# Loading the branch results into the place of their second part, and splitting them there

## The chip, the cores and the metric

The kernel runs on one core of a Trainium2 chip. The core has a matrix engine (TensorE, PE in the profile), a vector engine (DVE), a scalar engine (ACT), a general engine (POOL) and a sync engine (SP), which here issues nearly all transfers. Each engine works through its own list of instructions in order; semaphores join the lists. The metric is the device time of one execution in microseconds (us), lower is better: the median of three runs is 1705.68 us (1704.77 to 1709.62).

## The reference

The reference is one block of a network on 1024 tokens of width 1024. What matters here is its end:

```python
y_a = hm * jax.nn.sigmoid(a_o) * jax.nn.silu(a_z)               # first branch, [1024, 1024]
y_b = att.reshape(B, S, DA_WIDTH) * jax.nn.silu(b_z)            # second branch, [1024, 1024]
mix = (jax.nn.sigmoid(g_a + gb[0]) * jnp.einsum('bsc,cd->bsd', y_a, w_branch_a[layer])
       + jax.nn.sigmoid(g_b + gb[1]) * jnp.einsum('bsc,cd->bsd', y_b, w_branch_b[layer]))
x = x + jnp.einsum('bsd,de->bse', mix, w_out[layer])
return rmsnorm(x, final_g)
```

Before it stand a projection of the normed input, a gated recurrence (the first branch) and an attention with two softmaxes (the second).

## The kernel before, in words

All matrix products are made in three terms: each operand is split into a first part H, rounded to the short format that PE takes, and a second part L = value − H, and the product is H·H + H·L + L·H. So every operand needs a cast on ACT (H) and a subtraction on DVE or POOL (L).

Both branches leave their results transposed in device memory, as eight tiles of 128 features by 1024 tokens each: `yb0` to `yb7` for the second branch (in the profile `yb`, numbered 90 to 97) and `ya0` to `ya7` for the first (82 to 89). The **mixing** reads them back. `load_y` (L1310 to L1316) loads one tile of 512 KB into a tile `yraw`, which has two places in turn, takes two lasting places H and L, casts `yraw` to H on ACT (L1314) and subtracts on DVE (L1315). The lasting places are called `sl_yb` (a set of sixteen) and `sl_r` (another sixteen, in memory that the normed input `hH`, `hL` held until the last projection).

`mix_units` then makes eight output tiles per branch. For each, two halves of 512 tokens; each half is a group of 24 matmuls on PE (L429 in `proj`): for k from 0 to 7 the three terms with H and L of tile k. Two PSUM banks `pj` take turns. The branch b comes first ("pass B"), its groups are evicted by DVE at L1339; branch a follows ("pass A"). The places change hands: `ya0` to `ya3` go into `sl_r`, but `ya4` to `ya7` go into places of `sl_yb` that pass B has just finished with, and so do the first parts of the output matrix `w_out` (`load_wo`, from L1357), whose rows also come by way of the two places of `yraw`.

Around these loads other work shares the queues. The last gate products (`hH`, `hL` with `wH`, `wL`) run on PE until the mixing begins; ACT evicts them (L837, tile `gt`) and SP stores them (`tga`, 256 KB each). Every 10.9 us a weight tile `raw` (512 KB) is loaded, cast on ACT (L204, `wH`) and subtracted on POOL (L209, `wL`); the load of the next one waits for POOL. A tile `tgl` (512 KB) brings back the gate for each output tile.

PE's list is in the order in which the program writes it. The lists of SP, ACT, DVE and POOL in this stage are put in order when the program is built, by a scheduler that plans with its own costs and with what is free when; so a change to what a load waits for can move other instructions too. A transfer in SP's list that waits holds up all that stand behind it.

Of the kernel before, what the change touches and what calls it, by code (L numbers as in the profile page):

```python
# [7 lines left out]
F32 = mybir.dt.float32  # L8
# [6 lines left out]
S = 1024  # L15
# [4 lines left out]
L = 256  # L20
# [89 lines left out]
class Block:  # L110
# [1197 lines left out]


    def load_y(self, src, i, slot):  # L1310
        raw = self.wy.tile([128, S], F32, name="yraw", tag="yraw", bufs=2)
        self.q.dma_start(out=raw, in_=src[i])
        h, l = slot("H"), slot("L")
        self.a.copy(h, raw)  # L1314
        self.v.tensor_tensor(out=l, in0=raw, in1=h.bitcast(F32), op=ALU.subtract)  # L1315
        return h, l  # L1316

    def slot(self, which, dt=F32R):
        pool, bufs = {"yb": (self.wy, 16), "mb": (self.wy, 8), "r": (self.wr, 16)}[which]
        return pool.tile([128, S], dt, name="sl_" + which, tag=which, bufs=bufs)  # L1320
# [320 lines left out]
```

## Time and profile before

| what | value |
|---|---|
| median of three runs | 1705.68 us |
| the profiled execution's own time | 1706.56 us |
| its span, first to last instruction | 1704.7 us |
| PE busy | 1654.3 us, 97% |
| DVE, ACT, POOL busy | 988.3, 777.0, 606.5 us |
| mean granted TensorE clock | 0.994 |
| last matmul of the gate products starts at | 1426.42 us |
| first matmul of pass B starts at | 1427.42 us |
| first matmul of pass A starts at | 1521.95 us |

Times inside the execution count from the span's start. A row of the timeline has start, duration, engine, line, operation, output<-inputs, and in brackets the idle time before it with what ended that. A row of the stretches has their bounds and length, each engine's busy time with its count of instructions, the granted TensorE clock as a share of full speed, the transfer engines' busy share and the GB/s moved.

### The profile page before, as it was taken

How to read it: one execution, taken by the hardware profiler on the slowest of the kernel's cores; microseconds unless marked ns; L12 is line 12 of the kernel's file. 1: busy time of each engine (PE TensorE's matmuls, PEld its weight loads, DVE VectorE, ACT ScalarE, POOL GpSimd, SP SyncE). 2: the span in 40 equal slices, each digit the busy share in tenths (PEclk: the TensorE clock that was granted, in tenths of full speed). 3: DMA queues.
4: the chain of work that ended last, by engine and by line, in shares of the span. 5: the costliest groups of instructions: out<-in, count | busy, mean ns of one | idle time of the engine just before them, and what ended most of it. 6: DMA issues, size and time to landing. Idle time of an engine off the chain costs nothing. (4 is left out here: it accounts for less than half of the span.)

```text
span 1704.7 us, 25425 instructions
## 1 busy us (share of the span) xinstructions
PE 1654.3 (97%) x9431; PEld 1389.8 (82%) x9431; DVE 988.3 (58%) x1799; ACT 777.0 (46%) x1554; POOL 606.5 (36%) x680
## 2 busy tenths in 40 slices
PE   7999999999999999999999999999999899999998
PEld 5777887887877987898788878899999777888887
DVE  5778668674377666666666655226666633135533
ACT  7454555553265455454545455325655644022221
POOL 5767676665243134413241331221330312212000
PEclk9999999999999999999999999999999999999999
DMA  5334444334231213221231222175464327344222
GB/s 181 98 121 130 137 123 132 116 124 146 65 81 44 63 38 87 56 69 38 75 81 32 62 62 75 50 208 155 143 170 137 109 89 237 117 147 136 87 91 83
DMA packets 175630, 178.79 MB, mean 105 GB/s; under 512 B 12185, under 2 KB 135410, under 8 KB 175506
## 3 DMA queue, kind: packets, MB, share of 16 engines
q1 hardware_dynamic: 174594, 175.58, 34.5%
q8 instruction: 74, 1.21, 0.3%
q10 hardware_dynamic: 912, 1.59, 0.2%
q14 instruction: 50, 0.41, 0.1%
HBM read 114.11 MB, written 46.24 MB: 94 GB/s over the span
## 5 line engine op out<-in xcount | busy, mean ns | idle before, releaser
L429 PE MATMUL pj<-hH,wH 128*128 128x512 f32 x640 | 266.8, 417 | 3.3 <-ACT f L542 1.5
L429 PE MATMUL pj<-hH,wL 128*128 128x512 f32 x640 | 252.0, 394 | 1.8 <-POOL wL L207 1.8
L429 PE MATMUL pj<-hL,wH 128*128 128x512 f32 x640 | 250.8, 392 | 0.2 <-DVE hL L580 0.2
L209 POOL TENSOR_TENSOR wL<-raw,wH 128x1024 fp32r<-128x1024 f32 x41 | 99.7, 2431 | 291.9 <-ACT wH L204 289.5
L928 ACT ACTIVATE e<-S,nm 128x1024 f32<-128x1024 f32 x128 | 142.5, 1115 | 96.1 <-DVE nm L926 96.0
L926 DVE TENSOR_REDUCE nm<-S 128x1 f32<-128x1024 f32 x128 | 150.5, 1218 | 8.5 <-PE S L923 7.8
L429 PEld LDWEIGHTS pj<-hH,wH 128*128 128x128 f32 x640 | 121.0, 189 | 37.9 <-issue 14.5
L451 PE MATMUL pj<-wH,hH 128*128 128x256 f32 x512 | 149.9, 293 | 0.3
L948 DVE TENSOR_TENSOR pL<-T,pH 128x512 fp32r<-128x512 f32 x128 | 87.9, 689 | 105.8 <-ACT pH L947 104.9
L451 PE MATMUL pj<-wL,hH 128*128 128x256 f32 x512 | 144.8, 283 | 1.4 <-POOL wL L207 1.4
L429 PEld LDWEIGHTS pj<-hH,wL 128*128 128x128 f32 x640 | 120.6, 188 | 30.3 <-POOL wL L207 3.2
L451 PE MATMUL pj<-wH,hL 128*128 128x256 f32 x512 | 144.5, 282 | 0.0
L429 PEld LDWEIGHTS pj<-hL,wH 128*128 128x128 f32 x640 | 121.3, 190 | 18.3 <-DVE hL L580 0.6
L429 PE MATMUL pj<-sl_yb,wH 128*128 128x512 f32 x384 | 121.8, 397 | 4.4 <-ACT sl_yb L1314 2.2
L947 ACT CAST pH<-T 128x512 fp32r<-128x512 f32 x128 | 74.8, 585 | 84.6 <-PE T L131 84.0
L204 ACT CAST wH<-raw 128x1024 fp32r<-128x1024 f32 x56 | 58.9, 1052 | 114.3 <-PE pj L429 88.1
L923 PE MATMUL S<-kst,qq 64*128 64x512 f32 x768 | 106.7, 408 | 0.0
L451 PEld LDWEIGHTS pj<-wH,hH 128*128 128x128 f32 x512 | 97.7, 191 | 5.5 <-issue 2.2
L451 PEld LDWEIGHTS pj<-wL,hH 128*128 128x128 f32 x512 | 97.5, 190 | 2.3 <-POOL wL L207 2.3
L451 PEld LDWEIGHTS pj<-wH,hL 128*128 128x128 f32 x512 | 97.7, 191 | 0.1
L429 PEld LDWEIGHTS pj<-sl_yb,wH 128*128 128x128 f32 x384 | 73.3, 191 | 22.5 <-DVE sl_yb L1315 3.3
L923 PEld LDWEIGHTS S<-kst,qq 64*128 64x128 f32 x768 | 67.8, 184 | 26.3 <-issue 10.5
(358 smaller groups left out, 4112.2 us busy)
## 6 DMA issues: line engine op xcount, KB each, us to landing
raw<-in_w_in_dram SPq DMA_DIRECT2D x88, 512.0 KB, 3.9
kst<-hl SPq DMA_DIRECT2D x64, 128.0 KB, 2.4
qq<-hl SPq DMA_DIRECT2D x64, 128.0 KB, 2.4
x<-in_x_dram SPq DMA_DIRECT2D x8, 512.0 KB, 6.1
cak<-y SPq DMA_DIRECT2D x16, 256.0 KB, 2.3
cakH<-cin SPq DMA_DIRECT2D x16, 256.0 KB, 4.4
cakL<-tz SPq DMA_DIRECT2D x16, 256.0 KB, 4.1
gm<-oz SPq DMA_DIRECT2D x16, 256.0 KB, 2.7
```

The source lines that it names most:

```text
L204: self.a.copy(wH, raw)
L209: self.p.tensor_tensor(out=wL, in0=raw, in1=wHf, op=ALU.subtract)
L429: self.t.matmul(ps, lhsT=l[:, k, :], rhs=r, start=(n == 0), stop=(n == 23))
L451: self.t.matmul(ps[:, i, :], lhsT=l, rhs=r[:, k, :], start=(kh == 0 and k == 0 and m == 0), stop=(kh == 1 and k == 3 and m == 2))
L923: self.t.matmul(ps[:, o], lhsT=qq[r, x, c], rhs=k[r, y, o], start=(m == 0), stop=(m == 2))
L926: v.tensor_reduce(out=nm, in_=ps, axis=AX.X, op=ALU.max, negate=True)
L928: a.activation(out=e, in_=ps, func=AF.Exp, bias=nm[:, 0:1], accum_out=Z[:, j, t:t + 1])
L947: a.copy(pH[:, :, s], ps)
L948: v.tensor_tensor(out=pL[:, :, s], in0=ps, in1=pH[:, :, s].bitcast(F32), op=ALU.subtract)
```

## The change

`load_y` no longer has a tile `yraw`. It takes the two lasting places first, loads the tile straight into the place of L (seen as 32-bit floats), casts from there to H on ACT, and subtracts on DVE in place: L = L − H. `load_wo` is as before and now has the two places of `yraw` for itself until the output stage.

```diff
     def load_y(self, src, i, slot):
-        raw = self.wy.tile([128, S], F32, name="yraw", tag="yraw", bufs=2)
+
+        h, l = slot("H"), slot("L")
+        raw = l.bitcast(F32)
         self.q.dma_start(out=raw, in_=src[i])
-        h, l = slot("H"), slot("L")
         self.a.copy(h, raw)
         self.v.tensor_tensor(out=l, in0=raw, in1=h.bitcast(F32), op=ALU.subtract)
         return h, l
```

A load therefore waits for the place of its L, and no longer for the subtraction of the tile two before it. For `yb0` to `yb7` and `ya0` to `ya3` these places are free early. For `ya4` to `ya7` the place is that of L of `yb0` to `yb3`, which the last group of pass B still reads: each of these loads now waits for a matmul of that group. Lines after it stand one further down (L1314 is the load, L1315 the cast, L1316 the subtraction, L1367 the load of `w_out`).

The number of instructions on each engine stays; PE's list does not change but for the names of the tiles. The other lists move, at three places. The rows are: line, operation, output<-inputs, shape.

**SP, the loads of the second branch's tiles, from the fifth (`yb_94`) to the first of the next branch.** Before:

```order
L1312 DMA yraw<-yb_94 128x1024
L838 DMA tga_72<-gt 128x512
L1312 DMA yraw<-yb_95 128x1024
L838 DMA tga_73<-gt 128x512
L1312 DMA yraw<-yb_96 128x1024
L1312 DMA yraw<-yb_97 128x1024
L838 DMA tga_73<-gt 128x512
L173 DMA raw<-in_w_branch_b_dram 128x8x128
L1312 DMA yraw<-ya_82 128x1024
```

Now:

```order
L1314 DMA sl_yb<-yb_94 128x1024
L838 DMA tga_73<-gt 128x512
L1367 DMA yraw<-in_w_out_dram 128x1024
L1314 DMA sl_yb<-yb_95 128x1024
L1314 DMA sl_r<-ya_82 128x1024
L838 DMA tga_73<-gt 128x512
L1314 DMA sl_yb<-yb_96 128x1024
L173 DMA raw<-in_w_branch_b_dram 128x8x128
L1314 DMA sl_r<-ya_83 128x1024
L1314 DMA sl_yb<-yb_97 128x1024
```

The last three tiles of the second branch now stand behind a row block of `w_out` and two tiles of the first branch, `yb_97` also behind the weight `raw`, and `yb_95` and `yb_96` each behind a store of gates. Another row block of `w_out` stands further up, ahead of `yb_93`; and `yb_91` moved behind the weight `raw` that it was ahead of.

**ACT, the casts of the same tiles and what lies between them**, from the weight before the third cast on. Before:

```order
L204 CAST wH<-raw 128x1024
L1314 CAST sl_yb<-yraw 128x1024
L837 ACTIVATE gt<-pj,gbh 128x512
L1314 CAST sl_yb<-yraw 128x1024 x2
L837 ACTIVATE gt<-pj,gbh 128x512
L1314 CAST sl_yb<-yraw 128x1024
```

Now:

```order
L204 CAST wH<-raw 128x1024
L837 ACTIVATE gt<-pj,gbh 128x512
L1315 CAST sl_yb<-sl_yb 128x1024 x2
L837 ACTIVATE gt<-pj,gbh 128x512
L1315 CAST sl_yb<-sl_yb 128x1024
```

The second eviction shown used to have five casts ahead of it and has four now, since the eviction before it has moved ahead of the third cast. Further down (not shown) the casts into `sl_r` stand between those of the last three tiles of `sl_yb`.

**SP, the last tiles of the first branch, at the change from pass B to pass A.** Before (`ya_86` and `ya_87` stand some twelve rows further up):

```order
L173 DMA raw<-in_w_branch_a_dram 128x8x128
L1312 DMA yraw<-ya_88 128x1024
L1312 DMA yraw<-ya_89 128x1024
L1327 DMA tgl<-tga_67 128x1024
L173 DMA raw<-in_w_branch_a_dram 128x8x128
L1366 DMA yraw<-in_w_out_dram 128x1024 x4
```

Now:

```order
L173 DMA raw<-in_w_branch_a_dram 128x8x128
L1314 DMA sl_yb<-ya_86 128x1024
L1314 DMA sl_yb<-ya_87 128x1024
L1328 DMA tgl<-tga_67 128x1024
L1314 DMA sl_yb<-ya_88 128x1024
L173 DMA raw<-in_w_branch_a_dram 128x8x128
L1314 DMA sl_yb<-ya_89 128x1024
L1367 DMA yraw<-in_w_out_dram 128x1024 x3
```

All four loads now stand here; `ya_88` is behind the gate tile `tgl` and `ya_89` behind the weight `raw` as well, both of which they were ahead of.

## The prediction

> **What bounds the kernel now.** I read the page first, then the stretches of the mixing stage, then the chain of waits from its start to pass A. The page's first lines:
>
> ```profile
> span 1704.7 us, 25425 instructions
> PE 1654.3 (97%) x9431; PEld 1389.8 (82%) x9431; DVE 988.3 (58%) x1799; ACT 777.0 (46%) x1554; POOL 606.5 (36%) x680
> ```
>
> PE is the bound, so the change is worth what it does to PE's stops. The stretches of the stage (columns: bounds, length, busy time of PE, PEld, DVE, ACT, POOL, granted clock, share of the transfer engines, GB/s):
>
> ```profile
> 1410.00:1420.00 10.00, 10.00 (x46) 8.29 (x45) 3.44 (x2) 5.04 (x6) 2.40 (x1) 1.00 0.82 290
> 1430.00:1431.00 1.00, 1.00 (x7) 0.81 (x6) 0.00 (x0) 0.20 (x1) 1.00 (x1) 1.00 0.89 356
> 1430.00:1440.00 10.00, 6.58 (x20) 4.10 (x19) 3.14 (x3) 3.31 (x4) 2.17 (x1) 0.79 0.86 268
> 1432.36:1435.77 3.41, 1.23 (x3) 0.48 (x3) 1.23 (x1) 1.10 (x2) 0.00 (x0) 1.00 0.92 311
> 1435.77:1442.60 6.83, 6.14 (x14) 4.48 (x15) 3.58 (x4) 2.27 (x3) 0.00 (x0) 0.50 0.59 190
> 1442.60:1446.00 3.40, 3.40 (x16) 2.79 (x15) 0.79 (x2) 0.19 (x1) 0.00 (x0) 1.00 0.69 240
> 1460.00:1510.00 50.00, 50.00 (x223) 41.40 (x222) 6.19 (x9) 4.22 (x4) 9.77 (x5) 1.00 0.31 97
> ```
>
> There is one real stop, at the start of pass B. PE is busy for 1.23 of the 3.41 us before 1435.77, and then the clock stands at 0.50 for 6.83 us: with 6.14 us of matmuls in them that costs some 3.07 us more. Later, as in 1460 to 1510, PE never stops, so what is gained or lost at the stop reaches the end. The transfer engines are nearly full around the stop: 290, 268 and 311 GB/s at shares of 0.82 to 0.92. The chain of waits across the stop (start, duration, what):
>
> ```profile
> 1427.61 1.06 ACT sl_yb L1314
> ...
> 1428.69 1.24 DVE sl_yb L1315
> ...
> 1429.95 4.93 DMA yraw<-yb
> ...
> 1434.90 1.05 ACT sl_yb L1314
> ...
> 1435.98 1.24 DVE sl_yb L1315
> 1437.21 0.04 issue
> 1437.26 81.91 PE pj L429 x350
> ```
>
> This is the chain of two places: the sixth tile's subtraction frees a place of `yraw`, the eighth tile's load starts at 1429.95 and lands at 1434.88, cast and subtraction follow, and PE has k = 7's second part at 1437.26. The whole stop's size comes from these rows:
>
> ```profile
> 1426.42 0.39 PE L429 MATMUL pj<-hH,wL 128*128 128x512 f32 x1
> 1427.42 0.73 PE L429 MATMUL pj<-sl_yb,wH 128*128 128x512 f32 x2 [0.61 <-ACT gt L837]
> ...
> 1445.99 0.69 DVE L1339 SCALAR_TENSOR_TENSOR sl_mb<-tgl,pj 128x512 f32<-128x512 f32 x1 [2.61 <-PE pj L429]
> ...
> 1516.51 0.62 PE L429 MATMUL pj<-sl_yb,wH 128*128 128x512 f32 x2
> ...
> 1521.95 0.62 PE L429 MATMUL pj<-sl_r,wH 128*128 128x512 f32 x2
> ```
>
> A half, 24 matmuls, takes 1521.95 − 1516.51 = 5.44 us, 0.227 each. Without a stop the second half would be evicted 48 matmuls after 1426.42, at 1426.42 + 10.88 + 0.42 = 1437.7 (0.42 is one matmul's 0.39 and the start of DVE). It is evicted at 1445.99. So 8.3 us is all that better loads could win here.
>
> **The change: the work itself.** The same sixteen loads, casts and subtractions:
>
> ```profile
> L1312 SPq DMA_DIRECT2D yraw<-yb x8: 320/320/417, 1403.2 to 1429.9; - x8
> L1314 ACT CAST sl_yb<-yraw x8: 1041/1048/1057, 1407.1 to 1434.9; 128x1024 fp32r<-128x1024 f32 x8
> L1315 DVE TENSOR_TENSOR sl_yb<-yraw,sl_yb x8: 1216/1225/2630, 1408.2 to 1436.0; 128x1024 fp32r<-128x1024 f32 x8
> L1342 DVE TENSOR_TENSOR sl_mb<-sl_mb,tgl 128x512 f32<-128x512 f32 x16 | 12.9, 807 | 0.5
> L1341 DVE SCALAR_TENSOR_TENSOR tgl<-tgl,pj 128x512 f32<-128x512 f32 x16 | 11.0, 687 | 25.2 <-PE pj L429 25.2
> ```
>
> (The first three rows: one tile's instructions with shortest, median and longest in ns; the last two: groups with mean ns.) No row shows a subtraction of this shape in place. The nearest, L1342, is an addition in place: 807 ns mean for half the size, not faster and at most 17% slower than its neighbour L1341. I take 0, ends 0 and 0.2 us for each of the two on the path.
>
> **First place: pass B's tiles.** What the old chain made late is no longer tied to two places. But the new list of SP puts more ahead of the eighth tile: its own queue becomes the wait. (Timeline rows, and last a row of transfers issued, here `ya_88` and `ya_89`: count, size, median us to landing.) From the weight load at 1408.48 on:
>
> ```profile
> 1408.48 0.38 SPq L173 DMA_DIRECT2D raw<-in_w_branch_b_dram  x1
> 1408.95 0.53 SPq L1327 DMA_DIRECT2D tgl<-tgb  x1
> ...
> 1429.69 2.48 POOL L209 TENSOR_TENSOR wL<-raw,wH 128x1024 fp32r<-128x1024 f32 x1 [10.36 <-ACT wH L204]
> ...
> yraw<-ya SPq DMA_DIRECT2D x2, 512.0 KB, 3.5
> ```
>
> the list up to and with `yb_97` holds three `raw`, seven tiles of the second branch, two `tgl`, two blocks of `w_out` and two tiles of the first branch, sixteen loads of 0.524 MB, and four stores of 0.262 MB: 9.44 MB. A load alone lands 3.5 us after its issue, of which 1.8 us are its bytes at 290 GB/s, so bytes flow from about 1408.5 + 1.7 = 1410.2. At 311 GB/s, the rate of the stretch in which the engines were fullest, 9.44 MB take 30.4 us: `yb_97` lands at about 1440.6. No gap opens before that, by this replay: `yb_93` lands at 1410.2 + 3.93 MB / 311 = 1422.8, its cast and the eviction behind it release a store, and `w_out`, `yb_95` and `ya_82` issue at about 1425, while older bytes last to 1427.
>
> Cast (1.05) and subtraction (1.22) make k = 7's second part ready at 1442.9, 5.6 us later than the 1437.26 of before. From there 26 matmuls and the eviction's 0.4 take 6.3 us at full clock, and about 1.5 us more, since after so long a stop the half clock lasts to about 1446 (the stretches above change at steps of 3.41 us). Before it was 1445.99 − 1437.26 = 8.7. **Term: 5.6 + 7.8 − 8.7 = +4.7 us.**
>
> Bounds. At 356 GB/s, the best single microsecond, the load lands at 1436.7, k = 7 is ready at 1439.0, 1.7 late, and half clock to 1442.6 adds 1.8 to the 6.3: +1.1. At 268 GB/s it lands at 1445.4: 10.4 late, plus 6.3 and up to 1.7 of clock, less 8.7: +9.7. With an empty queue it still could not land early: it stands behind `raw`, which waits for POOL's `wL`, whose cast waits for the last gate matmul at 1426.2 + 0.4; 1.05 and 2.4 us later it is 1430.1, two more issues at 0.47 make 1431.0, after the old 1429.95. Landing 3.5 later, it would be ready at 1436.8: −0.4.
>
> The Trainium skill's "DMA: Bandwidth & Descriptors" (Specifications) gives about 358 GB/s as what one core gets from device memory. Only the one microsecond at 356 reaches that here; with it as the steady rate the term would be an estimated +1.
>
> **Second place: `ya4` to `ya7`.** Before, the first two tiles were split and the other two on their way when pass A began (timeline rows, a row of the tile `yraw`'s instructions with first and last start, and a row of transfers issued):
>
> ```profile
> 1521.97 1.05 ACT L204 CAST wH<-raw 128x1024 fp32r<-128x1024 f32 x1 [2.80 <-issue]
> ...
> 1522.15 0.69 DVE L1339 SCALAR_TENSOR_TENSOR sl_mb<-tgl,pj 128x512 f32<-128x512 f32 x1 [1.54 <-PE pj L429]
> ...
> 1523.10 2.41 POOL L209 TENSOR_TENSOR wL<-raw,wH 128x1024 fp32r<-128x1024 f32 x1 [8.48 <-ACT wH L204]
> ...
> 1526.64 0.50 PE L429 MATMUL pj<-sl_yb,wH 128*128 128x512 f32 x1 [0.22 <-DVE sl_yb L1315]
> ...
> 1527.77 0.50 PE L429 MATMUL pj<-sl_yb,wH 128*128 128x512 f32 x1 [0.17 <-DVE sl_yb L1315]
> ...
> L1312 SPq DMA_DIRECT2D yraw<-ya x2: 319/320/320, 1519.5 to 1520.6; - x2
> ...
> yraw<-in_w_out_dram SPq DMA_DIRECT2D x2, 512.0 KB, 5.4
> ```
>
> PE stopped for 0.22 and 0.17 us at k = 6 and 7; without these it reaches k = 7's second part at 1521.95 + 22 × 0.227 = 1526.9. Now the loads wait for matmuls of the last half (from 1516.51): `ya_86` issues at about 1517.1, `ya_87` at 1517.8; landing 3.5 us later they are in time for k = 4 and 5. Behind them in SP's list stands `tgl`, which waits for the last eviction (1522.15 before; now behind `ya_86`'s subtraction on DVE, about 1523.0 + 0.7), then `ya_88` at about 1524.1, then `raw`, which waits for POOL (1523.10 + 2.41 = 1525.5), then `ya_89` at about 1526.0. That is 5.4 us after the 1520.6 of before, and it goes out just behind a weight, where the two `w_out` loads needed 5.4 us to land: 1531.4. The four transfers from 1524 to 1526 at 311 GB/s would end at 1525.4 + 6.7 = 1532.1. I take 1531.8; cast and subtraction, 2.3: ready at 1534.1, 6.3 us after the 1527.77 of before. On ACT the cast of `ya_86` delays the weight cast behind it little, and a late bank of `pj` is wanted only 5.4 us later. A wait of this length, with few matmuls in it, should drop the clock as 1432.36 to 1435.77 did: 2.0 us more (half of some 4 us of matmuls). **Term: +8.3 us.** Ends: `ya_89` lands 3.5 us after its issue and the clock holds, 1529.5 + 2.3 − 1527.8 = +4.0; it lands at 1533.2 and the clock costs the full 3.3, +11.
>
> The skill's "TensorE: Matmul & The Clock Gate" (Part 1) says that the clock halves after one idle window of about 3.4 us and returns after one busy one. The length agrees with the 6.83 us here; but the window at 1432.36 had matmuls in it for 1.23 us and the clock fell all the same. If only a wholly idle window counted, this term would be +6.3.
>
> **Sum:** 4.7 + 8.3 = +13.0 us on the profiled span, 1704.7 to 1717.7. The profiled execution's own time lies 1.9 us above its span (1706.56) and 0.9 above the median (1705.68); the same added to the median gives **1718.7 us**.
>
> **The rivals.**
> 1. *The queue moves at its best rate* and `ya_89` lands as if alone. For it: the microsecond at 356. Against: no long stretch reaches it. Both low ends: +1.1 + 4.0, 1710.8 us.
> 2. *The queue is as slow as in 1430 to 1440*: 9.7 + 11, 1726.4 us.
> 3. *The first group keeps its clock.* `yb_95` and `yb_96` arrive so that no window is as empty as the one before 1435.77; the 3.07 us of half clock go, with the −0.4 of the empty queue, against +4.0 at the second place: 1706.2 us. Against: both tiles now issue behind evictions.
> 4. *The first stop goes*, the faster side: with eight places all loads run ahead, and k = 7 is ready when PE wants it, 1426.65 + 22 × 0.227 = 1431.6; from there on all 8.3 us are won. With `ya_89` also in time, 0.4 more: 1697.0 us. For it: the chain through `yraw` is what decides now. Against: `yb_97` cannot issue before 1431.0.
>
> That the change does not do what it says is excluded by the lists.
>
> **Chances:** the forecast 0.55, rival 1 0.22, rival 2 0.12, rival 3 0.07, rival 4 0.04. A measurement of this kernel tells a change from none at about 0.3%, 5.1 us. Slower: 0.55 + 0.12 and most of rival 1, 0.87. Within: rival 3 and the rest of 1, 0.08. Faster: 0.05. The range reaches from near rival 1's time to rival 2's: 1709 to 1727.
>
> **What would show it.** Right: PE in pass B's first group waits for k = 5, 6 and 7, the last of them till about 1443; the blocks of `w_out` and `sl_r` loads land ahead of `yb_97`; the load at 1430 to 1440 near 300 GB/s; in pass A's first group waits of some 7 us in all at k = 6 and 7, with the clock at 0.50 behind them; no new stop elsewhere. Wrong: k = 7 ready before 1437, or `ya_89` issued before `raw`; or a subtraction in place that is longer than 1.23 us.

## The result and the profile after

The changed kernel takes 1718.97 us (median of six runs, 1715.82 to 1721.3) against 1705.73 us before (six runs, 1704.77 to 1709.62). The ratio is **1.0073, with a 95% interval of 1.0058 to 1.0088**: slower by 0.7%, 13.2 us by the medians. The profiled execution took 1718.44 us, with a span of 1716.5 us, 11.8 us more than the span of before. Its page begins:

```profile
span 1716.5 us, 25419 instructions
...
PE 1655.9 (96%) x9431; PEld 1388.9 (81%) x9431; DVE 985.5 (57%) x1799; ACT 776.9 (45%) x1554; POOL 606.4 (35%) x680
```

The engines' busy times are those of before. What grew is what PE waits for, and this view (engine, line, what it waited for: us in total, times, longest) of the stretch from 1395 to 1580 has, beside 0.5 us that stand elsewhere, these two lines:

```profile
PE pj L429 <- ACT sl_yb L1315: 8.5, 5, 2.5
PE pj L429 <- DVE sl_yb L1316: 4.6, 6, 1.5
```

The same lines of before, which has another 0.6 us behind the last eviction of the gates:

```profile
PE pj L429 <- ACT sl_yb L1314: 2.2, 2, 1.4
PE pj L429 <- DVE sl_yb L1315: 1.6, 4, 0.8
```

All that grew is waiting for the casts and subtractions of the branches' tiles, at two places. PE's timeline, first pass B's first group, then pass A's:

```profile
1425.48 0.39 PE L429 MATMUL pj<-hH,wL 128*128 128x512 f32 x1
...
1434.46 0.80 PE L429 MATMUL pj<-sl_yb,wH 128*128 128x512 f32 x1 [1.84 <-ACT sl_yb L1315]
...
1439.37 0.79 PE L429 MATMUL pj<-sl_yb,wH 128*128 128x512 f32 x1 [2.43 <-ACT sl_yb L1315]
1440.63 0.80 PE L429 MATMUL pj<-sl_yb,wH 128*128 128x512 f32 x1 [0.46 <-DVE sl_yb L1316]
...
1525.21 0.62 PE L429 MATMUL pj<-sl_r,wH 128*128 128x512 f32 x2
...
1530.51 0.50 PE L429 MATMUL pj<-sl_yb,wH 128*128 128x512 f32 x1 [1.52 <-DVE sl_yb L1316]
1533.79 0.50 PE L429 MATMUL pj<-sl_yb,wH 128*128 128x512 f32 x1 [2.54 <-ACT sl_yb L1315]
...
1538.23 0.79 PE L429 MATMUL pj<-sl_yb,wH 128*128 128x512 f32 x1 [0.47 <-DVE sl_yb L1316]
```

In pass B's first group k = 7's second part is there at 1440.63, 15.15 us after the last gate matmul at 1425.48; before it was 1437.26 − 1426.42 = 10.84. In pass A's first group it is there 1538.23 − 1525.21 = 13.02 us after that pass's first matmul, before 5.82. The chain of waits that ends at the second place (start, duration, what), and SP's timeline of the same stretch:

```profile
1529.83 5.96 DMA sl_yb<-ya
...
1535.87 1.05 ACT sl_yb L1315
...
1536.94 1.24 DVE sl_yb L1316
```

```profile
1520.41 1.00 SPq L1314 DMA_DIRECT2D sl_yb<-ya  x2
1527.75 0.32 SPq L1328 DMA_DIRECT2D tgl<-tga  x1
1528.12 0.43 SPq L1314 DMA_DIRECT2D sl_yb<-ya  x1
1529.40 0.38 SPq L173 DMA_DIRECT2D raw<-in_w_branch_a_dram  x1
1529.83 0.58 SPq L1314 DMA_DIRECT2D sl_yb<-ya  x1
```

The first two tiles go out 4.8 us ahead of pass A; then SP stands still for over 6 us until the last eviction of pass B lets `tgl` go, and again until POOL lets `raw` go, and only then does the last tile leave.

To set kernels side by side I cut each span at the last gate matmul and at pass A's first matmul. The middle piece holds the first place and the rest of pass B, the last piece the second place and all that follows.

| span of the profiled execution | last gate matmul to pass A | pass A to the end |
|---|---|---|
| before, 1704.7 us | 95.5 | 182.8 |
| after, 1716.5 us | 99.7 (+4.2) | 191.3 (+8.6) |

The two pieces give +12.8; the rest of the 11.8, −0.9, lies ahead of the stage (the last gate matmul is at 1425.48 for 1426.42). In the profiles of the other kernels below that matmul starts anywhere from 1424.6 to 1426.2, so this may be the scatter of single executions; its cause stays open.

### The profile page after: what moved, and what is told of

It reads as the page before. It is cut to its first block, busy times and chain, and to the rows that moved or that the text cites. A ratio compares the mean times of both kernels' runs of the same rounds, so it can differ in the third digit from the quotient of the medians.

```text
span 1716.5 us, 25419 instructions
## 1 busy us (share of the span) xinstructions
PE 1655.9 (96%) x9431; PEld 1388.9 (81%) x9431; DVE 985.5 (57%) x1799; ACT 776.9 (45%) x1554; POOL 606.4 (35%) x680
```

## Experiments

My theory was that two places cost, independently, and both through the order of SP's list: at the first, what now stands ahead of `yb_97`; at the second, `tgl` and `raw` ahead of `ya_88` and `ya_89`. The rivals were that loading in place costs by itself, that the second stop only follows from the first, and that waiting for the place, not for the queue, makes the second term. Each kernel was compared with the kernel before on the same chip.

### Only the last four tiles in place

The other twelve go through `yraw` as before (diff against the changed kernel).

```diff
     def load_y(self, src, i, slot):
-        h, l = slot("H"), slot("L")
-        raw = l.bitcast(F32)
-        self.q.dma_start(out=raw, in_=src[i])
+        if src is self.ya and i >= 4:
+            h, l = slot("H"), slot("L")
+            raw = l.bitcast(F32)
+            self.q.dma_start(out=raw, in_=src[i])
+        else:
+            raw = self.wy.tile([128, S], F32, name="yraw", tag="yraw", bufs=2)
+            self.q.dma_start(out=raw, in_=src[i])
+            h, l = slot("H"), slot("L")
```

> Only ya4 to ya7 are loaded in place; yb0 to yb7 and ya0 to ya3 come by way of yraw as before, so the first group of pass B has the lists of before. If the two places are separate and the second is set by where ya_88 and ya_89 stand (behind tgl and behind raw): the first stop is that of before (k = 7 ready some 10.8 us after the last gate matmul), the second is whole, k = 7 ready about 13 us after pass A's first matmul where it was 5.8, and the time is 8 to 9 us over the kernel before, about 1714. Rival, the second stop is a result of the late first one (everything arrives late together): about 1706 to 1708.

Measured: 1715.3 us against 1705.36, ratio 1.0062 (1.0049 to 1.0076). PE's timeline of this kernel at the two places:

```profile
1437.03 0.80 PE L429 MATMUL pj<-sl_yb,wH 128*128 128x512 f32 x1 [0.77 <-DVE sl_yb L1320]
...
1520.54 0.61 PE L429 MATMUL pj<-sl_r,wH 128*128 128x512 f32 x2
...
1534.46 0.79 PE L429 MATMUL pj<-sl_yb,wH 128*128 128x512 f32 x1 [0.46 <-DVE sl_yb L1320]
```

The first place is that of before (10.87 us after its last gate matmul at 1426.16), and the second stop is whole: 1534.46 − 1520.54 = 13.9 us after pass A's start, and 192.9 us from there to the end, +10.1. So the second stop does not follow from the first, and it is the larger of the two. By the medians it is 9.9 us over the kernel before, more than the 8 to 9 expected: here the half clock lasted 10.24 us at the second place, in the changed kernel 6.83.

### The last four tiles ahead of the gates and the weight

`keep` names the engines whose lists stay in the order of the program; with SP among them from the loads of `ya4` to the output stage, these loads stand ahead of the first `tgl` of branch a and of its `raw`. The scheduler then also lets no block of `w_out` run ahead of them.

```diff
+            w.add(keep(E.PE, E.SP))
             w.add(*[do(lambda k=k: st3.__setitem__(("ga", k), self.load_y(self.ya, k, yb))) for k in range(4, 8)])
             passA = self.mix_units("ga", st3)
...
+            w.add(keep(E.PE))
             w.add(*self.out_units(st3))
```

> As the changed kernel, but from the loads of ya4 on SP's list is the program's order: ya_86 to ya_89 stand ahead of the first tgl of branch a and its raw (in this plan no block of w_out stands ahead of yb_97 either). If the place in SP's list makes the second term: the four loads go out when pass B's last half frees their places (from 1516.5 to 1519.3 in the times of before), land by 1526, k = 7 is ready within 1 us of before, and with the first place at -1 to +1 the time is 1704 to 1708. If the wait for the places alone makes it (the loads cannot go out before that half): second term +4 or more, 1710 or over.

Measured: 1707.93 us against 1705.36, ratio 1.0012 (1.0004 to 1.0021). SP's timeline and PE's:

```profile
1517.38 2.36 SPq L1314 DMA_DIRECT2D sl_yb<-ya  x4
1519.84 0.67 SPq L1328 DMA_DIRECT2D tgl<-tga  x1
```

```profile
1437.33 0.80 PE L429 MATMUL pj<-sl_yb,wH 128*128 128x512 f32 x1 [0.46 <-DVE sl_yb L1316]
...
1522.17 0.62 PE L429 MATMUL pj<-sl_r,wH 128*128 128x512 f32 x2
...
1529.14 0.50 PE L429 MATMUL pj<-sl_yb,wH 128*128 128x512 f32 x1 [0.17 <-DVE sl_yb L1316]
```

The four loads go out in one piece, in the last half of pass B, when their places come free; k = 7 is ready 6.97 us after pass A's start. The second term has fallen from 8.6 to 1.1 us (183.8 from pass A to the end). So the wait for the places costs 1.1 us at most, and the 7.5 us beside it came from where the loads stand in SP's list. At the first place, without `w_out` and with one tile of the first branch for two ahead of it, k = 7 comes 1437.33 − 1425.75 = 11.58 us after the last gate matmul, 3.6 us earlier than in the changed kernel. How these 3.6 us divide between the blocks of `w_out` and the tile stays open: a kernel that loads those blocks in place as well, which was to show it, has no time on record.

### Only the first twelve tiles in place

The same edit with the other condition, so that `ya4` to `ya7` go through `yraw`.

```diff
-        if src is self.ya and i >= 4:
+        if src is self.yb or i < 4:
```

> yb0 to yb7 and ya0 to ya3 in place, ya4 to ya7 by way of yraw; in SP's list ya_86 and ya_87 stand exactly where the changed kernel has its two blocks of w_out ahead of yb_97, so the same bytes lie ahead of it. If the bytes ahead make the first term whatever they are: k = 7 in pass B's first group as late as in the changed kernel (about 15 us after the last gate matmul, before 10.8), first term +4, no stop at pass A (four tiles are on chip long before): +4 to +5 against before, about 1709.5. If it is something in the blocks of w_out themselves: first term near 0, 1705 or less.

Measured: 1708.92 us against 1704.86, ratio 1.0022 (1.0013 to 1.003). SP's list around `yb_97`, and PE's timeline:

```profile
1430.40 0.38 SPq L173 DMA_DIRECT2D raw<-in_w_branch_b_dram  x1
1430.88 0.53 SPq L1314 DMA_DIRECT2D sl_r<-ya  x1
1431.46 0.51 SPq L1314 DMA_DIRECT2D sl_yb<-yb  x1
```

```profile
1440.12 0.79 PE L429 MATMUL pj<-sl_yb,wH 128*128 128x512 f32 x1 [0.47 <-DVE sl_yb L1320]
```

With other loads in the same places of the list, k = 7 is late again: 1440.12 − 1425.60 = 14.5 us after the last gate matmul, where the changed kernel has 15.2. And at pass A nothing is left of the second term (182.7 us to the end, 182.8 before). So it is not something in the blocks of `w_out` themselves: other loads in their places do it as well. By the medians this place alone costs 4.1 us (1708.92 − 1704.86); in the profiled execution, 0.8 us below its median, the middle piece shows +2.4, with 10.24 us of half clock for the changed kernel's 13.65.

### One place for the blocks of w_out

The first line is in `load_wo`, the second in the output stage.

```diff
-            raw = self.wy.tile([128, D], F32, name="yraw", tag="yraw", bufs=2)
+            raw = self.wy.tile([128, D], F32, name="yraw", tag="yraw", bufs=1)
...
-            sq = self.wy.tile([128, D], F32, name="sqo", tag="yraw", bufs=2)
+            sq = self.wy.tile([128, D], F32, name="sqo", tag="sqo", bufs=2)
```

> As the changed kernel, but one place of yraw for the blocks of w_out (the output stage's squares get their own two places); one block of w_out stands ahead of yb_97 for two, all else in SP's list up to pass A is the same. By bytes at 311 to 322 GB/s yb_97 lands 1.6 us earlier than in the changed kernel: k = 7 about 13.5 us after the last gate matmul, time 1.5 to 3 us under the changed kernel (the half clock may end one step earlier), about 1716.5; the second place as in the changed kernel. If yb_97 is bound by its issue behind raw: no change, 1719.

A miss: 1724.99 us against 1704.86, ratio 1.011 (1.0095 to 1.0126), slower than the changed kernel. Its PE timeline at the first place and in the output stage, and the stretch of half clock at the second place:

```profile
1439.56 0.79 PE L429 MATMUL pj<-sl_yb,wH 128*128 128x512 f32 x1 [0.46 <-DVE sl_yb L1316]
...
1631.94 0.50 PE L1400 MATMUL pj<-sl_r,sl_yb 128*128 128x512 f32 x1 [3.46 <-ACT sl_r L1370]
```

```profile
1530.65:1544.30 13.65, 8.39 (x18) 5.41 (x18) 5.84 (x8) 4.53 (x7) 0.00 (x0) 0.50 0.37 134
```

The edit had a cost of its own that the expectation left out: with one place the last block of `w_out` comes late, PE stops for 3.5 us in the output stage, and the clock halves behind it. At the second place nearly the same wait (7.0 us for 5.9) was followed by 13.65 us of half clock where the changed kernel had 6.83. At the first place k = 7 came 14.6 us after the last gate matmul, 0.6 earlier than in the changed kernel, not 1.6. So the run as a whole says little; its first place says, in the one execution profiled, that one block fewer is worth less than its bytes.

### The whole change, with SP's list in program order

```diff
+            w.add(keep(E.PE, E.SP))
             yb = lambda x: self.slot("yb")
             loads = [do(lambda k=k: st3.__setitem__(("gb", k), self.load_y(self.yb, k, yb)), 1.0) for k in range(8)]
...
+            w.add(keep(E.PE))
             w.add(*self.out_units(st3))
```

> The changed kernel with SP's list in the order of the program from the loads of yb on to the output stage: yb_97 ahead of the tgl and of the last raw, nothing of w_out or of the first branch ahead of it, ya_86 to ya_89 ahead of the first tgl of branch a. If loading in place costs nothing by itself and only the order does: yb_97 goes out at about 1422.5, lands by 1428, k = 7 is ready at about 1430.5, when PE wants it; first stop gone (-8.3), the second place +1.1 as in the run with the last four ahead: 1697 to 1700. If loading in place costs by itself (subtractions over 1.23, loads that wait for the place): 1704 or more.

Measured: 1700.33 us against 1704.86, ratio 0.9967 (0.9955 to 0.998). The same loads in place are now faster than the kernel before, though 0.3 us above the range expected. SP's row with the last two tiles of the second branch, a stretch, and the tile's instructions (shortest, median, longest in ns):

```profile
1421.85 0.93 SPq L1314 DMA_DIRECT2D sl_yb<-yb  x2
```

```profile
1430.00:1440.00 10.00, 9.01 (x37) 6.85 (x38) 4.23 (x5) 1.46 (x2) 0.00 (x0) 1.00 0.65 212
```

```profile
L1316 DVE TENSOR_TENSOR sl_yb<-sl_yb x8: 1210/1218/2635, 1407.3 to 1431.6; 128x1024 fp32r<-128x1024 f32 x8
```

`yb_97` leaves at about 1422.3, the clock keeps 1.00, and the median subtraction is no longer than through `yraw`. So loading in place costs nothing by itself that these rows show. Some 1.2 us of waits are left at each place. At the first, 0.9 of them are for one subtraction that took 2.59 us (from 1428.00) while POOL's `wL` ran (1427.10 to 1429.51). The rest is DVE's pace: PE gets the last three subtractions 1.13 us apart, and uses up a tile in 3 × 0.227 = 0.68.

### The kernel before, with four and with three places

Nothing is loaded in place here; `yraw` has more places (the same lines with 3 in the second run).

```diff
-        raw = self.wy.tile([128, S], F32, name="yraw", tag="yraw", bufs=2)
+        raw = self.wy.tile([128, S], F32, name="yraw", tag="yraw", bufs=4)
...
-            raw = self.wy.tile([128, D], F32, name="yraw", tag="yraw", bufs=2)
+            raw = self.wy.tile([128, D], F32, name="yraw", tag="yraw", bufs=4)
...
-            sq = self.wy.tile([128, D], F32, name="sqo", tag="yraw", bufs=2)
+            sq = self.wy.tile([128, D], F32, name="sqo", tag="yraw", bufs=4)
```

> The kernel before with four places of yraw for two, nothing else. The scheduler then puts all eight yb loads ahead of the first tgl and of the second raw. If the load chain through the places is what bounded the first stop of the kernel before: yb_97 lands by about 1426, k = 7 is ready when PE wants it, up to 8.3 us are won: about 1698, at least 4 us. If the stop has another cause behind it (casts queued behind evictions, the weight now later in the queue): less than 2 us, 1704 to 1706.

> The kernel before with three places of yraw. Only one raw (ahead of yb_93) and one tgl ahead of yb_97, which can go out when the subtraction of yb_94 is done, by about 1421 to 1423: lands by 1428, the first stop almost gone as with four places: 1697 to 1700. If three places still bind (the chain load 3.5 to 5, cast 1.05, subtraction 1.22 per three tiles): a stop of 2 to 4 us remains, 1700 to 1703.

Measured: with four places 1696.95 us against 1705.36, ratio **0.9949** (0.9937 to 0.9962); with three 1697.8 against 1704.86, ratio 0.9952 (0.994 to 0.9965). These are the fastest kernels of the study, faster than before and after. For four places, SP's row with the last two tiles of the second branch, the stretches, and all of PE's waits from 1395 to 1700:

```profile
1417.86 0.88 SPq L1312 DMA_DIRECT2D yraw<-yb  x2
```

```profile
1430.00:1440.00 10.00, 10.00 (x46) 8.28 (x45) 4.62 (x5) 4.77 (x5) 0.58 (x1) 1.00 0.86 296
...
1520.00:1530.00 10.00, 10.00 (x46) 8.29 (x45) 6.45 (x9) 2.32 (x3) 2.72 (x1) 1.00 0.75 253
```

```profile
PE T L131 <- ACT hm L1216: 0.5, 1, 0.5
```

`yb_97` leaves at 1418.3 and PE does not stop at either place. From the last gate matmul to pass A it is 1512.51 − 1425.25 = 87.3 us, 8.3 less than before: the whole of the stop, as the prediction had sized it from the rows of before.

## Why the prediction was right, and where it was not

The time was forecast at 1718.7 us and is 1718.97. The mechanism holds at both places. That the two times agree to 0.3 us is luck in part: errors inside the terms cancel, and six executions of the changed kernel spread over 5.5 us.

**What bounds the kernel: right.** The first stop was worth 8.3 us, and the run with four places won 8.3 between the last gate matmul and pass A.

**First place, +4.7 forecast, +4.2 measured.** The mechanism held: what stands ahead of `yb_97` in SP's list makes it late. Two sizes were off. The transfers ran faster than the 311 GB/s I took (a view of the transfers from 1409 to 1439):

```profile
DMA packets 5663, 10.14 MB, mean 338 GB/s; under 512 B 333, under 2 KB 3303, under 8 KB 5663
```

so the tile's cast could start at 1438.3 (1439.37 less the cast's 1.05), 12.8 us after the last gate matmul where the forecast's 1440.6 is 14.2 after it, and k = 7 came 4.3 us late, not 5.6. The trace of before already had faster stretches than the two that I took for its fullest and its best (311 GB/s at a share of 0.92, and a microsecond at 356):

```profile
1413.50:1418.00 4.50, 4.50 (x21) 3.75 (x20) 0.22 (x1) 2.25 (x3) 1.07 (x1) 1.00 0.99 375
```

So 356 was no upper bound of the rate, and the low end of this term was not worked out from the best one. On the other side, I let the stretch from k = 7 to the eviction shrink by 0.9 us (7.8 for 8.7); it took 1449.25 − 1440.63 = 8.6. The end of the half clock, about 1446, was right:

```profile
1432.09:1445.75 13.66, 8.47 (x18) 5.14 (x17) 7.40 (x7) 5.22 (x5) 0.00 (x0) 0.50 0.54 199
...
1449.25 0.69 DVE L1340 SCALAR_TENSOR_TENSOR sl_mb<-tgl,pj 128x512 f32<-128x512 f32 x1 [5.54 <-PE pj L429]
```

The transfer itself was only half of the cause. Against the run with the last four ahead, where k = 7 came 3.6 us earlier, the lateness splits into three parts by SP's rows of both, the changed kernel's first:

```profile
1430.60 0.38 SPq L173 DMA_DIRECT2D raw<-in_w_branch_b_dram  x1
...
1431.65 0.92 SPq L1314 DMA_DIRECT2D sl_yb<-yb  x1
```

```profile
1429.57 0.38 SPq L173 DMA_DIRECT2D raw<-in_w_branch_b_dram  x1
1430.00 0.57 SPq L1314 DMA_DIRECT2D sl_yb<-yb  x1
```

`raw`, which `yb_97` stands behind, goes out 5.12 us after the last gate matmul, there 3.82 (1.3 us); `yb_97` follows it by 1.05 us, there 0.43, since a tile of the first branch stands between (0.6); and it takes 6.6 us to land, there 4.9 (1.7). The first part goes by way of ACT: the cast of a tile that landed late stands ahead of the weight's, POOL's `wL` starts late, and `raw` with it (the changed kernel's ACT):

```profile
1426.03 1.05 ACT L1315 CAST sl_yb<-sl_yb 128x1024 fp32r<-128x1024 f32 x1 [3.02 <-DMA sl_yb<-yb]
1426.99 1.04 ACT L204 CAST wH<-raw 128x1024 fp32r<-128x1024 f32 x1
```

The prediction had this weight in its lower bound for an empty queue, but with its cast on time.

**Second place, +8.3 forecast, +8.6 measured.** Here the path holds step by step. The first two loads go out 4.8 us ahead of pass A, as forecast (1517.1 for 1521.95). But the cast of `ya_86` began 4.4 us after its issue (1520.41 to 1524.82), not 3.5, and what stands behind it moved along: the eviction on DVE, `tgl` and the weight's cast. So `ya_89` goes out 4.6 us after pass A's start (forecast 4.05); it takes 5.96 us to land (5.8), and k = 7 is 7.2 us later than before (6.3). The half clock costs the remaining 1.4 (2.0). One statement was wrong: that `ya_86` and `ya_87` are in time for k = 4 and 5. PE waited 1.52 us for the second of them, whose subtraction ran beside POOL's `wL` (1526.90, 2.48 us):

```profile
1527.80 2.66 DVE L1316 TENSOR_TENSOR sl_yb<-sl_yb 128x1024 fp32r<-128x1024 f32 x1
```

It did not set when k = 7 came: the chain above leads there from the load of `ya_89`.

**The subtraction in place at 0: right.** Alone it takes 1.22 to 1.23 us, as through `yraw`. By the letter, one sign of being wrong came: a subtraction in place longer than 1.23 us, the one of 2.66. But it is not a matter of the place: in the kernel before the longest through `yraw` took 2.63 us, it too while POOL's `wL` ran (1416.93 to 1419.33).

**The rivals.** The best rate (rival 1) failed at its low ends: the transfers were faster than in the forecast, but the first place was held by the weight too, and `ya_89` did not land as if alone. The slow queue and the kept clock did not come. Rival 4, that the whole first stop goes, has the right mechanism for another kernel: it needs `yb_97` to go out early, which four places of `yraw` or another order of SP's list give, and this change does not. With four places the time is 8.4 us below the kernel before, where that rival had put 8.7.

**Not foreseen:** the 0.9 us ahead of the stage, with which the span came to +11.8 for +13.0.

## What to carry to other kernels

Freeing a load from the buffers that it waited for also frees every other load that shared them: where a scheduler orders the queue, read in the new list what now runs ahead of the load that the bottleneck waits for. When loads are given places that come free late, look at what the queue puts between them: at the second place the wait for the places cost at most 1.1 us, and two unrelated transfers ahead of the last loads cost 7.5. If a chain through two places bounds a stage, try a third place before taking the places away; it cost 4 KB of each partition here and won 0.5%.

## What the runs showed of the hardware

**The clock.** The granted clock changes at steps of 3.41 us, and a step at half speed follows a step in which PE was too little busy, not idle: in the changed kernel the clock fell after a step with 1.48 of 3.42 us of matmuls and after one with 0.68, and held after one with 1.89. In the kernel with one place for the blocks of `w_out` it fell after steps with 1.70 and 1.64.

```profile
1428.67:1432.09 3.42, 1.48 (x6) 0.66 (x4) 1.84 (x2) 2.09 (x2) 1.90 (x1) 1.00 0.88 281
...
1438.92:1442.33 3.41, 2.49 (x5) 1.70 (x6) 3.29 (x4) 2.49 (x3) 0.00 (x0) 0.50 0.24 99
...
1527.66:1531.07 3.41, 1.89 (x8) 1.05 (x7) 2.73 (x2) 0.10 (x1) 1.72 (x1) 1.00 0.63 216
1531.07:1534.49 3.42, 0.68 (x2) 0.19 (x1) 0.72 (x1) 1.04 (x1) 0.00 (x0) 1.00 1.00 343
```

A step with 2.49 us of matmuls at half clock was followed by another at half. This suggests that a stop costs by how it lies to these steps: at the second place waits of 5.9, 6.6 and 7.0 us were followed by 6.83, 10.24 and 13.65 us of half clock in three kernels, which differ by far more than the waits. Kernels without these stops also scatter less: five runs with four places lie within 1.8 us, six of the changed kernel within 5.5. That the steps cause this scatter was not tested. The Trainium skill's "TensorE: Matmul & The Clock Gate" (Part 1) has the clock halve after one idle window of about 3.4 us; the length agrees with these rows, "idle" does not.

**The transfers.** In the changed kernel 375 GB/s flowed for 10 us, as they did for 4.5 us in the kernel before, and both are over the 356 of the microsecond in the prediction:

```profile
1410.00:1420.00 10.00, 10.00 (x46) 8.29 (x45) 3.18 (x3) 4.07 (x5) 2.44 (x1) 1.00 1.01 375
```

The Trainium skill's "DMA: Bandwidth & Descriptors" (Specifications) gives about 358 GB/s as what one core gets from device memory; this row is above it, and so is that of the kernel before, where more than the prediction's one microsecond reached it.
